# Block-product chunks: where the down slabs stand, where the raw blocks lie, and which sums a transfer makes

## The chip, the core and the metric

The kernel runs on one core of a Trainium2 chip. The core has a matrix engine (PE, with its weight loads shown apart as PEld), a vector engine (DVE), a scalar engine (ACT), a general engine (POOL) and a queue engine (SP) that here only issues transfers. Sixteen DMA engines move data between the chip's memory and the core's SBUF. The metric is the device time of one execution in microseconds. A program's instructions stand in one fixed order on each engine; engines wait for each other on semaphores.

## The reference

Two layers are computed on 256 tokens of width 1024, in float32. Each layer is a feed-forward part, a mixer (short convolution, recurrence, pooling), cross attention to 256 memory rows, and a second feed-forward part, each followed by a normalisation:

```
def swiglu(x, w_gate, w_up, w_down):
    return (jax.nn.silu(x @ w_gate) * (x @ w_up)) @ w_down
...
for l in range(DEPTH):
    h = layer_norm(ALPHA * h + 0.5 * swiglu(h, ffn1_gate[l], ffn1_up[l], ffn1_down[l]), ...)
    ... mixer, cross attention ...
    h = layer_norm(ALPHA * h + 0.5 * swiglu(h, ffn2_gate[l], ffn2_up[l], ffn2_down[l]), ...)
```

The gate and up weights are 1024 x 2816, the down weights 2816 x 1024. So there are four feed-forward parts, and they are what the change touches.

## The kernel before

**Products.** To keep float32 accuracy with the faster float32r matmul, each operand is split into a high part and a rest: `split` copies the value to float32r on ScalarE (L61) and subtracts it on VectorE (L62). A product is three matmuls, high by high, high by rest, rest by high (`mm_rows`, L112 by `product`). Weights come by transfers from SP into tiles of 128 x 1024 numbers with the tag `raw` (six of them) and are split into tiles `whi` and `wlo`, eight of each.

**A feed-forward part** (`ffn`) goes over the 2816 columns in five chunks of 512 and one of 256. For a chunk it computes gate and up, applies silu, multiplies, and turns the result (`turn`: four transfers named `dealt` that move it between partitions, two vector transposes at L458, one more split into `ah` and `al`). The chunk's result is then multiplied with rows of the down weights. Those come as two slabs of 256 rows for each chunk; `both(c, u)` makes the 24 matmuls of slab u of chunk c, into four PSUM banks that stay open for the whole part. The slabs lag behind: around chunk c stand `both(c - 2, 1)` and `both(c - 1, 0)`.

**Block products.** Chunks 2, 3 and 4 of a part (only 3 and 4 of the first part of layer 0, where other work is done at the start: `sevens`) are computed by `by_seven`. The chunk is seen as a 2 by 2 product: token halves by halves of the 1024 inner rows, times the gate block and the up block, each in two halves of rows: `w00` and `w10` are the gate's first and second half, `w01` and `w11` the up's. Seven products of blocks instead of eight give the result. Some of them take sums of blocks: the sums of x are made once a part (`blocks_of_x`, `bx`), the sums of weight blocks in each chunk, in place in the raw tiles, by `parts_of(r, plus)` at L606: two VectorE additions of 128 x 1024 for a block. Each product (`run`) has 12 matmuls. In this order the kernel before makes: x00 by w00; bx0 by w00+w01; bx1 by that plus w11; (x01) by w10; bx2 by w01+w11; then `between()`, which is `both(c - 2, 1)`; bx3 by w11; x11 by the sum of all four. Three sums are thus made: the first two add into w00 on VectorE, the third adds w11 into w01 on VectorE. The fourth block of the last sum, w10, is added into w00 by accumulating transfers from POOL's queue (L644): they read the gate's second half from memory again and add it to what lies in SBUF. After the seventh product stands `both(c - 1, 0)`, and then `left()`: silu of the second token half, the last subtraction, the gating product at L664, and `turn`.

Results of products are taken from PSUM by `taken` (a ScalarE copy, L635) and `put` (a VectorE operation, L625).

**Where raw blocks lie.** A block needs two raw tiles. Besides the six shared `raw` tiles there are `spare0`, `spare1` and `spare2` of the part's own pool, and `lng` and `lnb`, which hold normalisation parameters at the end of each part. Chunks alternate: w00 lies in the spares and w01 in lng/lnb, or the other way round; w11 takes two shared tiles, w10 `spare2` and one shared tile. A load into a tile is issued from SP when the last reader of the tile's old content is done, and SP's loads are issued in one order.

**What sets the order.** The code is recorded by a framework that keeps the order of dependent work and orders each engine's instructions by its own estimates of when they can start. So an engine's order is fixed in the built program, but isn't the code's line by line; the order of PE is nearly that of the code, while VectorE and ScalarE go ahead into the next products and into the next chunk as far as the eight tiles of split weights let them.

Of the kernel before, what the change touches and what calls it, by code (L numbers as in the profile page):

```python
# [12 lines left out]
ALU = mybir.AluOpType  # L13
# [4 lines left out]
P = 128  # L18
# [10 lines left out]
CHUNK = 512  # L29
# [17 lines left out]
def model(ctx: ExitStack, tc: tile.TileContext, t: dict, out: bass.AP):  # L47
    nc = tc.nc
# [5 lines left out]
    def acc(shape=(P, 2, SEQ), tag="acc"):  # L54
        return ps.tile(list(shape), F32, tag=tag, name=tag)
# [351 lines left out]
    def ffn(l, name, n, pend=None, last=False, early=None):  # L407
        gate, up, down = (t[f"{name}_{x}"][l] for x in ("gate", "up", "down"))
        with tc.tile_pool(name="ffn", bufs=2, reuse_waits="tile") as fp:
# [165 lines left out]
            def by_seven(c0, bx, between):  # L575
# [19 lines left out]
                homes = [("spare0", "spare1"), ("lng", "lnb")]  # L595
                turn_of = sevens.index(c0 // CHUNK) % 2
                w00 = block(gate, 0, pieces(*homes[turn_of]))
                w01 = block(up, 0, pieces(*homes[1 - turn_of]))
                w11 = block(up, 1, pieces("raw", "raw"))
                w10 = block(gate, 1, pieces("spare2", "raw"))  # L600

# [28 lines left out]
                s = activations()  # L630
# [6 lines left out]
                o = [acc((P, CHUNK)) for _ in range(2)]  # L637
                run(o[0], part_of_x(0, 0), parts_of(w00))
                taken(s[:, 0, :], o[0])
                run(o[1], bx[0], parts_of(w00, w01))  # L640
                run(o[0], bx[1], parts_of(w00, w11), True)
                for i in range(2):
                    k = 4 + 2 * i
                    nc.gpsimd.dma_start(  # L644
                        w00[i], gate[k * P : (k + 2) * P, c0 : c0 + CHUNK].rearrange("(k p) c -> p k c", p=P),
                        accum_op=ALU.add,
                    )
                taken(e, o[0])
                o.append(acc((P, CHUNK)))
                run(o[2], part_of_x(0, 1), parts_of(w10))  # L650
                run(o[0], bx[2], parts_of(w01, w11), True)
                put(s[:, 0, :], o[2], ALU.add, s[:, 0, :])
                nc.scalar.activation(s[:, 0, :], s[:, 0, :], AF.Silu)
                taken(f, o[0])
                between()
# [71 lines left out]
            for c, (c0, ncol) in enumerate(chunks):  # L727
# [3 lines left out]
                elif c in sevens:  # L731
                    left = by_seven(c0, bx, lambda: both(c - 2, 1))
# [16 lines left out]
                if c > 0:  # L749
                    if c > 1 and c not in sevens:  # L750
                        both(c - 2, 1)
                    if c < len(chunks) - 1:
                        both(c - 1, 0)
                    if c in sevens:
                        acts.append(left())
            end = [slab(4, 0), slab(4, 1), slab(5, 0)]
# [479 lines left out]
```

## Time and profile before

| | |
|---|---|
| Median of three runs | 1084.16 us (1083.94 to 1084.78) |
| The profiled execution | 1086.89 us |
| Its span, first to last instruction | 1085.2 us |
| Granted TensorE clock, mean | 0.997 |
| Busy: PE, DVE, ACT, POOL | 1059.0, 969.0, 669.1, 91.5 us |
| Read from memory | 227.69 MB |

The page gives for each group of instructions its line and engine, what it writes and reads, how often it stands, its busy time, the mean of one in ns, and the idle time before it with what ended it. The chain of waits follows the work that ended last back to the start. The windows give busy times inside stretches of the span. Matmuls are pipelined, so a matmul's own time overlaps the next one's; how far apart their starts are tells their price.

### The profile page before, as it was taken

What the parts mean: (1) busy time and instruction counts of PE and PEld (TensorE: products, weight loads), DVE (VectorE), ACT (ScalarE), POOL (GpSimd) and SP (SyncE); (2) the same over time, 40 slices, a digit from 0 to 9 for tenths busy, and PEclk for the clock granted to TensorE, in tenths of its full rate; (3) what the DMA queues carried; (4) which work ended last, traced back from release to release, by engine and by line L of the source; (5) the groups of instructions that cost most, each with busy time, mean ns of one, the idle gap of its engine ahead of it and who ended that gap; (6) DMA issues with size and microseconds to landing.
All of it is one profiled execution on the core that took longest, in us unless ns stands there. A gap on an engine that the chain in (4) does not pass through costs nothing.

```text
span 1085.2 us, 16259 instructions
## 1 busy us (share of the span) xinstructions
PE 1059.0 (98%) x5918; PEld 927.8 (85%) x5918; DVE 969.0 (89%) x1279; ACT 669.1 (62%) x920; POOL 91.5 (8%) x136
## 2 busy tenths in 40 slices
PE   9998999999999999999999999999999999999997
PEld 7887788989899888888888887888898998888786
DVE  6979987998998799999899999888989788999996
ACT  7547675767457566567575677666764655667661
POOL 9600001000000000000000000010000000000000
PEclk9999999999999999999999999999999999999999
DMA  9997595755575587679776787957536664786691
GB/s 361 266 290 209 160 322 181 254 195 166 165 271 176 177 278 201 209 259 268 237 276 191 270 271 190 300 181 241 182 131 210 240 238 166 252 271 192 196 291 40
DMA packets 136882, 243.45 MB, mean 224 GB/s; under 512 B 9761, under 2 KB 48961, under 8 KB 136801
## 3 DMA queue, kind: packets, MB, share of 16 engines
q1 hardware_dynamic: 129024, 228.49, 62.4%
q0 software_dynamic: 7200, 12.73, 7.0%
q10 hardware_dynamic: 576, 1.18, 0.3%
q8 instruction: 46, 0.75, 0.3%
q14 instruction: 36, 0.29, 0.1%
HBM read 227.69 MB, written 1.05 MB: 211 GB/s over the span
## 4 chain that ended last, share of the span: by engine, by line
PE 69%; DVE 15%; DMA 7%; issue 5%; ACT 3%; SPq 0%; DVEq 0%; ACTq 0%
PE acc L112 45%; PE dn L112 21%; DVE wlo L62 8%; DMA raw<-in_ffn_up_dram 3%; DMA raw<-in_ffn_gate_dram 3%; DVE raw L606 3%; ACT whi L61 2%; DMA dealt<-sg 1%; PE acc L179 1%; DVE square L458 1%; DVE sg L664 1%; PE dn L938 1%; DVE al L62 1%; DVE sg L445 0%; SPq L455 0%
## 5 line engine op out<-in xcount | busy, mean ns | idle before, releaser
L61 ACT CAST whi<-raw 128x1024 fp32r<-128x1024 f32 (+1 forms) x462 | 463.7, 1041 | 184.4 <-DVE raw L606 79.0
L62 DVE TENSOR_TENSOR wlo<-raw,whi 128x1024 fp32r<-128x1024 f32 (+1 forms) x462 | 542.5, 1207 | 27.2 <-ACT whi L61 24.4
L112 PE MATMUL acc<-whi,xT 128*128 128x512 f32 x872 | 268.5, 381 | 5.0 <-ACT whi L61 4.8
L112 PEld LDWEIGHTS acc<-whi,xT 128*128 128x128 f32 x872 | 164.9, 189 | 30.5 <-ACT whi L61 7.4
L112 PE MATMUL acc<-wlo,xT 128*128 128x512 f32 x436 | 165.8, 380 | 3.5 <-DVE wlo L62 3.5
L112 PE MATMUL acc<-xT,whi 128*128 128x512 f32 x576 | 142.2, 382 | 0.2
L112 PE MATMUL dn<-whi,ah 128*128 128x512 f32 x346 | 130.1, 381 | 1.4 <-ACT whi L61 1.4
L112 PE MATMUL dn<-wlo,ah 128*128 128x512 f32 x346 | 131.4, 380 | 0.0
L112 PE MATMUL dn<-whi,al 128*128 128x512 f32 x346 | 131.1, 379 | 0.0
L112 PEld LDWEIGHTS acc<-xT,whi 128*128 128x128 f32 x576 | 104.0, 190 | 12.5 <-ACT whi L61 0.7
L112 PEld LDWEIGHTS acc<-wlo,xT 128*128 128x128 f32 x436 | 82.4, 189 | 16.8 <-DVE wlo L62 5.4
L112 PE MATMUL dn<-whi,xT 128*128 128x512 f32 x288 | 87.8, 381 | 0.0
L606 DVE TENSOR_TENSOR raw<-raw 128x1024 f32<-128x1024 f32 x66 | 78.7, 1215 | 1.7 <-DMA raw<-in_ffn_up_dram 1.6
L112 PEld LDWEIGHTS acc<-xT,wlo 128*128 128x128 f32 x576 | 75.5, 191 | 3.9
L112 PE MATMUL acc<-xT,wlo 128*128 128x256 f32 x576 | 75.9, 275 | 0.0
L112 PEld LDWEIGHTS dn<-whi,ah 128*128 128x128 f32 x346 | 65.1, 189 | 12.0 <-ACT whi L61 3.0
L112 PE MATMUL acc<-whi,kTh 128*128 128x512 f32 x176 | 68.5, 389 | 5.8 <-ACT sg L635 3.8
L112 PEld LDWEIGHTS dn<-wlo,ah 128*128 128x128 f32 x346 | 65.4, 189 | 10.0 <-DVE wlo L62 0.9
L112 PEld LDWEIGHTS dn<-whi,al 128*128 128x128 f32 x346 | 65.4, 189 | 9.2
L112 PE MATMUL acc<-wlo,kTh 128*128 128x512 f32 x176 | 67.7, 385 | 0.8 <-DVE wlo L62 0.8
L112 PE MATMUL acc<-whi,kTl 128*128 128x512 f32 x176 | 67.5, 383 | 0.0
L112 PEld LDWEIGHTS dn<-whi,xT 128*128 128x128 f32 x288 | 54.4, 189 | 7.7 <-DVE xT L62 0.3
(235 smaller groups left out, 1297.0 us busy)
## 6 DMA issues: line engine op xcount, KB each, us to landing
raw<-in_ffn_up_dram SPq DMA_DIRECT2D x88, 512.0 KB, 5.8
raw<-in_ffn_down_dram SPq DMA_DIRECT2D x88, 512.0 KB, 5.7
raw<-in_ffn_gate_dram SPq DMA_DIRECT2D x84, 512.0 KB, 5.3
raw<-in_w_in_dram SPq DMA_DIRECT2D x48, 512.0 KB, 4.7
raw<-in_ffn_gate_dram POOLq DMA_DIRECT2D x22, 512.0 KB, 6.4
dealt<-sg SPq DMA_DIRECT2D x80, 128.0 KB, 3.2
raw<-in_ca_k_dram SPq DMA_DIRECT2D x16, 512.0 KB, 4.9
raw<-in_w_out_dram SPq DMA_DIRECT2D x16, 512.0 KB, 4.4
```

The lines of the kernel that those rows point to most:

```text
L61: nc.scalar.copy(hi, src)
L62: lows.append(nc.vector.tensor_tensor(lo, src, hi.bitcast(F32), op=ALU.subtract))
L112: nc.tensor.matmul(o, w, x, start=start, stop=stop, skip_group_check=more)
L179: nc.tensor.transpose(pt[:, k, :], src[:, (4 * j + k) * P : (4 * j + k + 1) * P], unit)
L458: nc.vector.transpose(d[:, i].rearrange("p k (b r) -> p b k r", b=4), x[:, :, i, :].rearrange("p b (k j) -> p b k j", k=4),)
L606: nc.vector.tensor_tensor(r[i], r[i], plus[i], op=ALU.add)
L664: nc.vector.tensor_tensor(s, s, ef, op=ALU.mult)
L938: nc.tensor.matmul(o[g, hh, :], kc[:, hh, g], x, start=True, stop=True)
```

## The change

Four things change inside `by_seven` and around it.

1. The third sum, w01 + w11, is no longer made on VectorE. A function `more` issues accumulating transfers; it is used for w00 as before, and now also for w01: after the sum w00 + w01 has read it, two transfers from POOL's queue add the up's second half into it.
2. The order of products. x01 by w10 now stands third, into its own bank that is there from the start, and bx1 by w00+w01+w11 fourth. The next slab product `both(c - 2, 1)` then stands between the fourth product and bx2 by w01+w11, which add to one bank; and `both(c - 1, 0)` stands between that one and bx3 by w11. `left()` follows the seventh product at once.
3. The raw blocks lie in three homes by turns, the spares, lng/lnb and two shared tiles, so that w00, w01 and w11 move on by one home from chunk to chunk.
4. The gate's second half (w10) is loaded ahead of the up's second half (w11).

The number of matmuls, of splits and of plain loads is the same.

```diff
-                homes = [("spare0", "spare1"), ("lng", "lnb")]
-                turn_of = sevens.index(c0 // CHUNK) % 2
-                w00 = block(gate, 0, pieces(*homes[turn_of]))
-                w01 = block(up, 0, pieces(*homes[1 - turn_of]))
-                w11 = block(up, 1, pieces("raw", "raw"))
+                homes = [("spare0", "spare1"), ("lng", "lnb"), ("raw", "raw")]
+                n = sevens.index(c0 // CHUNK)
+                w00 = block(gate, 0, pieces(*homes[n % 3]))
+                w01 = block(up, 0, pieces(*homes[(n + 1) % 3]))
                 w10 = block(gate, 1, pieces("spare2", "raw"))
+                w11 = block(up, 1, pieces(*homes[(n + 2) % 3]))
...
-                o = [acc((P, CHUNK)) for _ in range(2)]
+                o = [acc((P, CHUNK)) for _ in range(3)]
                 run(o[0], part_of_x(0, 0), parts_of(w00))
                 taken(s[:, 0, :], o[0])
+                def more(to, m, j):
+                    for i in range(2):
+                        k = 4 * j + 2 * i
+                        nc.gpsimd.dma_start(
+                            to[i], m[k * P : (k + 2) * P, c0 : c0 + CHUNK].rearrange("(k p) c -> p k c", p=P),
+                            accum_op=ALU.add,
+                        )
+
                 run(o[1], bx[0], parts_of(w00, w01))
+                more(w01, up, 1)
+                run(o[2], part_of_x(0, 1), parts_of(w10))
                 run(o[0], bx[1], parts_of(w00, w11), True)
-                for i in range(2):
-                    k = 4 + 2 * i
-                    nc.gpsimd.dma_start(
-                        w00[i], gate[k * P : (k + 2) * P, c0 : c0 + CHUNK].rearrange("(k p) c -> p k c", p=P),
-                        accum_op=ALU.add,
-                    )
+                more(w00, gate, 1)
+                put(s[:, 0, :], o[2], ALU.add, s[:, 0, :])
                 taken(e, o[0])
-                o.append(acc((P, CHUNK)))
-                run(o[2], part_of_x(0, 1), parts_of(w10))
-                run(o[0], bx[2], parts_of(w01, w11), True)
-                put(s[:, 0, :], o[2], ALU.add, s[:, 0, :])
+                between[0]()
                 nc.scalar.activation(s[:, 0, :], s[:, 0, :], AF.Silu)
+                run(o[0], bx[2], parts_of(w01), True)
                 taken(f, o[0])
-                between()
+                between[1]()
                 put(f, o[1], ALU.subtract, f)
                 run(o[1], bx[3], parts_of(w11), True)
                 run(o[0], part_of_x(1, 1), parts_of(w00), True)
...
-                    left = by_seven(c0, bx, lambda: both(c - 2, 1))
+                    left = by_seven(c0, bx, [lambda: both(c - 2, 1), lambda: both(c - 1, 0)])
...
-                    if c > 1 and c not in sevens:
-                        both(c - 2, 1)
-                    if c < len(chunks) - 1:
-                        both(c - 1, 0)
                     if c in sevens:
                         acts.append(left())
+                    else:
+                        if c > 1:
+                            both(c - 2, 1)
+                        if c < len(chunks) - 1:
+                            both(c - 1, 0)
```

## The prediction

> **What bounds the kernel now.** I read the page first, for the busiest engine and the chain of waits, then the windows of the stretches that the change touches, then the timeline inside them.
>
> ```profile
> span 1085.2 us, 16259 instructions
> PE 1059.0 (98%) x5918; PEld 927.8 (85%) x5918; DVE 969.0 (89%) x1279; ACT 669.1 (62%) x920; POOL 91.5 (8%) x136
> PE 69%; DVE 15%; DMA 7%; issue 5%; ACT 3%; SPq 0%; DVEq 0%; ACTq 0%
> ```
> ```profile
> 161.29 18.13 PE dn L112 x84
> ```
> TensorE is the bound, and no matmul is taken away or added. The chain's undisturbed run gives the price of a 128x512 matmul, 18.13 / 84 = 0.2158 us. What can be won is only what PE loses. A block-product chunk has seven products of 12 matmuls and two down slabs of 24, so 132 x 0.2158 = 28.5 us. These windows run from the first matmul of a feed-forward part's first such chunk to the last matmul of its last one (two chunks in the first part, three in the others):
>
> ```profile
> 85.79:150.65 64.86, 59.47 (x266) 50.83 (x264) 64.54 (x76) 46.73 (x53) 4.85 (x4) 0.97 0.74 223
> 421.25:512.60 91.35, 87.90 (x398) 74.11 (x397) 88.44 (x85) 64.10 (x73) 5.95 (x5) 1.00 0.82 248
> 592.17:684.25 92.08, 87.92 (x397) 74.11 (x396) 88.91 (x86) 63.96 (x73) 5.99 (x5) 1.00 0.82 245
> 954.85:1046.27 91.42, 87.93 (x397) 74.11 (x396) 89.52 (x86) 63.92 (x73) 5.96 (x5) 1.00 0.81 247
> ```
> Columns after the length: busy PE, PEld, DVE, ACT, POOL, then clock, share of the DMA engines, GB/s. Against 264 x 0.2158 = 57.0 and 396 x 0.2158 = 85.5 us, PE loses 7.9, 5.9, 6.6 and 6.0: 26.4 us together, the ceiling of any gain. Who takes them: the timeline of PE, and the chain between 440 and 492 us.
>
> ```profile
> 94.49 0.48 PE L112 MATMUL acc<-whi,kTh 128*128 128x512 f32 x1 [3.35 <-ACT sg L635]
> 96.27 0.63 PE L112 MATMUL acc<-whi,kTh 128*128 128x512 f32 x1
> 96.70 0.63 PE L112 MATMUL acc<-wlo,kTh 128*128 128x512 f32 x1
> 457.85 0.48 PE L112 MATMUL acc<-wlo,xT 128*128 128x512 f32 x1 [0.96 <-DVE wlo L62]
> 659.54 0.48 PE L112 MATMUL acc<-whi,xT 128*128 128x512 f32 x1 [2.01 <-ACT whi L61]
> ```
> ```profile
> by line: DVE wlo L62 38.8%; issue 19.8%; DMA raw<-in_ffn_up_dram 11.3%; DVE raw L606 10.1%; DMA raw<-in_ffn_gate_dram 8.6%; DVE square L458 4.8%; DVE sg L664 4.7%; PE acc L112 3.1%; DVE al L62 2.2%; ACT whi L61 2.0%; DVE halves L625 1.3%; D
> ```
> PE waits for the splits of weights into hi and lo, and their chain is VectorE's: splits (L62) and block sums (L606). After the longest wait ten matmuls came 0.43 us apart, so that one cost some 2 us more.
>
> **The change part by part.** First VectorE's price of a chunk.
>
> ```profile
> L606 DVE TENSOR_TENSOR raw<-raw 128x1024 f32<-128x1024 f32 x66 | 78.7, 1215 | 1.7 <-DMA raw<-in_ffn_up_dram 1.6
> ```
> ```profile
> 498.82 0.68 DVE L625 TENSOR_TENSOR halves<-acc,halves 128x512 f32<-128x512 f32 x1
> 499.42 6.89 DVE L62 TENSOR_TENSOR wlo<-raw,whi 128x1024 fp32r<-128x1024 f32 x6
> ```
> ```profile
> 457.72 1.30 DVE square L458 x2
> ```
> Large instructions follow each other at (6.89 - 1.22) / 5 = 1.135 us, those from PSUM at 0.60, the two transposes take 1.3. Now a chunk has 6 sums, 14 block splits, 4 slab splits, the gating product and one split of the activations: 26 x 1.135 + 3 x 0.60 + 1.3 = 32.6 us, 4.1 above PE. With the third sum made by transfers it is 24, or 30.3 us: 1.85 above PE. VectorE is still the slower one, but starts ahead. What it starts with is read from the loss: 3 x 4.1 - 5.9 = 6.4 us (5.7 and 6.3 in the later parts). Three chunks then use up 5.6 of it, and the loss is gone. In the first part 7.9 less 2 of slow clock is 5.9, so the start is 8.2 - 5.9 = 2.3; two chunks need 3.7, and 1.4 stays.
>
> The order. Until now five products come before the first slab, with 16 of the large instructions against 60 matmuls (18.2 against 12.9 us); then four products, 12 against 48 (13.6 against 10.4), and each slab (2.3 against 5.2) lets VectorE catch up sooner. In the built program the split of the earlier chunk's activations, which the second slab now needs before the sixth product, stands behind 21 large instructions, three small and the transposes, 27 us into VectorE's chunk, and PE is there after 5 x 2.59 + 5.18 = 18.1. So 8.8 us of lead are needed. Eight buffers of split weights let VectorE be up to the splits of the second sum ahead (13 large, two small, 16 us in the new order), so 7.2 are to spare against 5.6 used. I book no gain for the order, since the loss is used up already.
>
> ```profile
> q1 hardware_dynamic: 129024, 228.49, 62.4%
> q0 software_dynamic: 7200, 12.73, 7.0%
> raw<-in_ffn_up_dram SPq DMA_DIRECT2D x88, 512.0 KB, 5.8
> raw<-in_ffn_gate_dram POOLq DMA_DIRECT2D x22, 512.0 KB, 6.4
> ```
> ```profile
> L644 POOL DMA_DIRECT2D raw<-in_ffn_gate_dram x22 | 26.4, 1202 | 385.8 <-DVE wlo L62 385.8
> ```
> ```profile
> DMA to landing us min/median/max: 5.6/6.4/8.9
> ```
> ```profile
> DMA to landing us min/median/max: 3.6/5.8/8.3
> ```
> The last two are of the accumulating transfers (L644) and of the chunks' raw loads (L590).
> The transfers. 22 more accumulating ones. POOL's issue (1.2 us each) is free: it waits 385.8 us in that place. The gate block's transfers stand behind the up block's on that queue, whose last is released by a sum that VectorE does some seven instructions earlier. In the built order ten large instructions, two small and the transposes (13.8 us) lie between the sum that last reads the up block and its split, and ten, one and the transposes (13.2) between the second sum's split and the last product's; the slowest landing took 8.9, so both are hidden, with 4 us to spare. On the engines one costs at most 7.0% of 1085.2 us / 22 = 3.45 us of all sixteen (the queue carries other things too) and at least what a plain one costs, 62.4% x 1085.2 / 228.49 MB x 0.524 = 1.55. I take 3.1, near the upper row, since those are the same transfers.
>
> Homes. The up block of a next chunk no longer lies where the last product's weights were, but where the up block's second half was. Its buffer comes free one product earlier; in a third chunk five large VectorE instructions and a small one (6.3 us) lie between that and its sum, against a landing of 5.8. At 8.3 it would be 2 us late, at 3.6 not at all: I take 1 us in each part for this and for restarts, 4 in all. The gate's second half is loaded ahead of the up's, as it is now used first. The third bank is taken from the start: four exist, three were used, no cost. The gating starts right after the seventh product, with the next chunk's first product as cover (2.6 us against 0.6 of activation for the bank); behind the gating multiply queue the next chunk's later splits, which wait for buffers then anyway; without that cover 1 us a chunk.
>
> Sum: 26.4 - 1.4 - 4 = 21.0 us. The profiled execution took 1086.89 (1.7 around its span), the median of the runs is 1084.16, 2.7 less: 1065.9 profiled, 1063.2 for the median.
>
> **The rivals.**
>
> ```profile
> 430.00:442.00 12.00, 11.48 (x53) 9.75 (x52) 11.44 (x11) 9.27 (x11) 0.00 (x0) 1.00 1.05 407
> 445.00:454.00 9.00, 9.00 (x43) 7.87 (x43) 9.00 (x9) 2.69 (x3) 0.57 (x1) 1.00 0.25 61
> 490.00:496.00 6.00, 5.74 (x25) 4.48 (x25) 6.00 (x7) 6.00 (x8) 1.20 (x1) 1.00 1.03 173
> 492.00:524.00 32.00, 32.00 (x164) 27.90 (x163) 29.42 (x30) 22.12 (x28) 0.00 (x0) 1.00 0.99 308
> ```
> One: the DMA engines become the bound. The second part's 0.82 x 91.35 = 74.9 us get 6 x 3.1 more: 93.5. At the highest share seen, 1.05, that is 89.1 us, not 85.5; the three long parts win 2.3, 3.0 and 2.3, the first 7.4, and the time is 1069. At 0.99 it is 94.4 us, each long part loses 3 and the kernel ends near 1089. For it: accumulates alone fill the engines (1.03) at 173 GB/s. Against it: the engines stand at 0.25 where the new ones start, and at 0.99 for 32 us PE lost nothing.
> The Trainium skill ("DMA: Bandwidth & Descriptors", Issuing engines are not separate DMA queues) says that transfers from every queue run on the same 16 engines and interleave, which speaks for this rival; the trace agrees, 1.05 at most for both queues together. By the same page's fit (Anatomy of one DMA, 2.0 us and bytes at 436 GB/s) an accumulate would hold them 1.2 us as an estimate, and the second part would need 82.1 / 1.05 = 78.2, no bound; the trace's 173 GB/s for accumulates alone contradicts that.
>
> Two, slower: the second slab waits. It stands two products earlier and needs the earlier chunk's activations, whose way is:
>
> ```profile
> 418.43 2.62 SPq L455 DMA_DIRECT2D dealt<-sg  x4
> ```
> ```profile
> dealt<-sg SPq DMA_DIRECT2D x80, 128.0 KB, 3.2
> ```
> ```profile
> L61 ACT CAST ah<-square 128x1024 fp32r<-128x1024 f32 x20 | 20.9, 1046 | 14.1 <-DVE square L458 14.1
> L441 ACT ACTIVATE sg<-acc 128x512 f32<-128x512 f32 x27 | 15.9, 594 | 23.0 <-PE acc L112 22.0 <-DMA dealt<-sg 0.9
> ```
> Activation 0.6, multiply 1.2, issues 2.6, landing 3.2, transposes 1.3, cast 1.0, split 1.2: 11.1 us against PE's 18.1. It decides if the lead never reaches 8.8: from 26.4 / 11 = 2.4 us of wait a chunk on, the kernel is slower, and a wait as long as the 3.35 seen also slows the clock. At 3.5 a chunk: +38.5 - 26.4, or 1096.
> Three, nothing moves: PE's waits are for loads, so VectorE's sums don't matter. The chain's 20% of raw loads speak for it, L606 in the same chain against it: 1084.
>
> **How the numbers follow.** Forecast 0.60 (own range 1059 to 1068, from no slip to a slip of 2 us in each part more); DMA-bound and still faster 0.15 (1069 to 1081); no change, that is within 0.2% or 2.2 us, which is what a measurement of this kernel can tell, 0.05; DMA-bound at 0.99 0.07 (1089); waiting slab 0.13 (1096). Faster 0.75, same 0.05, slower 0.20. The range goes from 1058, all 26.4 us won, to 1087, short of the slower cases.
>
> **What would show it.** L606 x44, VectorE's busy time 27 us less, 44 accumulates, the software queue near 24.3 MB; the long parts' windows at 86 to 87.5 us and the first at 58 to 60, DMA share there 0.95 and above. Landings of raw loads over 7 us in the median, or new PE waits of dn matmuls for the activations' splits, would make it wrong.

## The result and the profile after

The changed kernel takes 1078.73 us (median, 1078.14 to 1081.95), the kernel before 1084.88 us (1083.94 to 1087.26) on the same chip: the ratio is 0.9946, with a 95% interval of 0.993 to 0.9962. It is faster by 4 to 8 us. The forecast was 1063.2 us, a gain of 21 us; the direction came, less than a third of the size did.

The page of the changed kernel: the span, the busy engines, the chain by engines, the software queue, the sums and the accumulating transfers.

```profile
span 1076.9 us, 16377 instructions
PE 1056.5 (98%) x5918; PEld 925.8 (86%) x5918; DVE 947.1 (88%) x1257; ACT 671.2 (62%) x920; POOL 119.0 (11%) x158
q0 software_dynamic: 13184, 24.27, 13.2%
PE 69%; DVE 14%; DMA 6%; issue 6%; ACT 5%; SPq 1%; DVEq 0%; ACTq 0%
L606 DVE TENSOR_TENSOR raw<-raw 128x1024 f32<-128x1024 f32 x44 | 53.0, 1218 | 0.4
raw<-in_ffn_up_dram POOLq DMA_DIRECT2D x22, 512.0 KB, 6.0
raw<-in_ffn_gate_dram POOLq DMA_DIRECT2D x22, 512.0 KB, 7.9
```

The profiled execution took 1078.62 us, within 0.1 us of the median of its kernel; that of before had been 2 us above its own. What was to be removed is removed: 22 additions fewer, 44 accumulating transfers, 24.27 MB in the software queue. VectorE is 22 us less busy, where 27 were forecast. TensorE's share did not move, as it was the bound already.

The windows of the same four stretches, from the first matmul of a part's first block-product chunk to the last of its last one (columns as in the prediction: length, PE, PEld, DVE, ACT, POOL, clock, DMA share, GB/s):

```profile
85.49:147.87 62.38, 58.48 (x265) 49.49 (x264) 60.47 (x72) 46.63 (x53) 7.15 (x6) 1.00 0.94 265
419.45:508.47 89.02, 86.92 (x398) 74.37 (x396) 84.26 (x81) 62.14 (x71) 11.95 (x10) 1.00 0.98 269
588.48:677.08 88.60, 86.92 (x397) 74.30 (x396) 83.88 (x80) 61.57 (x69) 11.91 (x10) 1.00 0.98 270
948.29:1036.90 88.61, 86.93 (x398) 74.30 (x397) 83.88 (x80) 61.34 (x70) 11.91 (x10) 1.00 0.98 268
```

Against the floors of 57.0 and 85.5 us TensorE (264 and 396 matmuls of 0.2158 us) now loses 5.4, 3.6, 3.1 and 3.1 us, 15.2 in all where it was 26.4: 11.2 us are won here. The span fell by 8.3 only, so some 3 us came back outside. The distances between the stretches show where: from the end of one to the start of the next it was 270.60, 79.57 and 270.60 us, and is 271.58, 80.01 and 271.21; from the end of the last one to the end of the span it was 38.9 us and is 40.0. Right behind each stretch stands a new wait: matmuls of a down slab need the activations (ah) of the 256-column chunk. In the kernel before, a slab still stood behind the seventh product, and these activations were ready in time. At the four places the matmuls' starts now lie 1.0, 0.4, 0.4 and 1.2 us further apart than the price of a matmul, 3.0 us together; before, no start there was late. The waits of TensorE, and its timeline at the first of these places:

```profile
PE dn L112 <- ACT whi L61: 3.3, 4, 0.9
PE dn L112 <- DVE wlo L62: 2.6, 7, 1.0
PE acc L112 <- ACT halves L635: 1.8, 2, 1.6
PE acc L112 <- ACT sg L635: 1.6, 4, 0.8
PE dn L112 <- ACT ah L61: 0.9, 2, 0.6
```
```profile
167.93 0.48 PE L112 MATMUL dn<-whi,ah 128*128 128x512 f32 x1 [0.36 <-ACT ah L61]
```

The rows of waits give the sum in us, the number and the longest. Those for the activations sum to 0.9 us, less than the 3.0 above, since a wait is counted here only from 0.1 us on and the matmul after it is late too. No wait is long, and four kinds remain: for the cast of slab weights, for their split, for the copies that ScalarE makes of the products' banks (L635, `taken`), and for the activations behind the stretch.

The first two are the largest, 5.9 us. In the third chunk of the second part:

```profile
486.94 1.13 PE L112 MATMUL dn<-whi,ah 128*128 128x512 f32 x4 [0.80 <-ACT whi L61]
484.90 4.84 ACT L61 CAST whi<-raw 128x1024 fp32r<-128x1024 f32 x5 [4.17 <-DVE raw L606]
```

The slab's cast stands on ScalarE behind the cast of a block sum, and ScalarE has stood idle for 4.17 us until VectorE had made that sum. VectorE in turn waits 1.17 us for the cast before it can split. All four of TensorE's waits for casts of slab weights stand right behind such an idle time of ScalarE, of 4.17 to 5.40 us. So VectorE sets the pace there without being busy throughout. No run takes this hand-over away by itself, so what it is worth is not shown.

One more thing is only in the trace. The written order puts the first slab between the fourth product and the fifth. In the built program, from the second block-product chunk of a part on, 13 to 16 of that slab's 24 matmuls stand ahead of the fourth product: the scheduler filled a gap with them. Which gap, the timeline of TensorE shows in the second such chunk of the second part, where 0.76 us of it are left:

```profile
459.43 0.38 PE L112 MATMUL dn<-whi,ah 128*128 128x512 f32 x1
460.56 0.48 PE L112 MATMUL acc<-whi,kTh 128*128 128x512 f32 x1 [0.76 <-ACT sg L635]
```

The fourth product adds to the bank of the first, so it waits until ScalarE has copied that bank into the tile `sg`. This became the centre of the study.

### The profile page after: what moved, and what is told of

The parts are those of the page before. It is cut to its first block, busy times and chain, and to the rows that moved or that the text cites. A ratio compares the mean times of both kernels' runs of the same rounds, so it can differ in the third digit from the quotient of the medians.

```text
span 1076.9 us, 16377 instructions
## 1 busy us (share of the span) xinstructions
PE 1056.5 (98%) x5918; PEld 925.8 (86%) x5918; DVE 947.1 (88%) x1257; ACT 671.2 (62%) x920; POOL 119.0 (11%) x158
## 3 DMA queue, kind: packets, MB, share of 16 engines
q0 software_dynamic: 13184, 24.27, 13.2%
## 4 chain that ended last, share of the span: by engine, by line
PE 69%; DVE 14%; DMA 6%; issue 6%; ACT 5%; SPq 1%; DVEq 0%; ACTq 0%
PE acc L112 47%; PE dn L112 20%; DVE wlo L62 6%; ACT whi L61 4%; DMA dealt<-sg 2%; DVE raw L606 2%; DMA raw<-in_ffn_gate_dram 1%; DMA raw<-in_ffn_up_dram 1%; PE acc L179 1%; SPq L455 1%; DVE square L458 1%; DMA raw<-in_ffn_down_dram 1%; DVE sg L668 1%; PE dn L943 1%; ACT ah L61 0%
## 5 line engine op out<-in xcount | busy, mean ns | idle before, releaser
L357 POOL TENSOR_TENSOR rs<-rs,nhalf 128x1 f32<-128x1 f32 x16 | 14.9, 933 | 434.0 <-DVE rs L353 307.1
```

The lines of the kernel that those rows point to most:

```text
L357: nc.gpsimd.tensor_tensor(rs, rs, nhalf[:, 0:1], op=ALU.pow)
```

## The experiments

All times are medians; ratios are to the kernel before on the same chip, with 95% intervals. The kernel before took 1084.9 to 1086.2 us beside the various runs, so differences between two changed kernels are taken from their ratios.

**First round: three suspicions.** Theory A was that the order built for TensorE, with slab matmuls ahead of the fourth product, costs what is missing; B that the DMA engines became full; C that the cover lost behind the stretches costs it. The first kernel holds TensorE to the written order:

```
+                    with tc.manual_schedule(engines={E.PE}):
-                    left = by_seven(c0, bx, [lambda: both(c - 2, 1), lambda: both(c - 1, 0)])
+                        left = by_seven(c0, bx, [lambda: both(c - 2, 1), lambda: both(c - 1, 0)])
```

> The changed kernel, with PE's instructions of each block-product chunk kept in the order in which they are written: in the changed kernel the built order puts 13 to 16 of the first slab's matmuls ahead of the fourth product in second and third chunks. Theory A (PE's built order asks for the slab's splits and for the fourth product's bank sooner than VectorE and ScalarE deliver them): the long parts' stretches fall from 89.0, 88.6 and 88.6 us to 87 or less and the first from 62.4 to 60 or less, the time by 4 to 8 us against the changed kernel, to 1071 to 1075. Theory B (the DMA engines, 0.98 busy there, set the pace): the stretches keep within 0.7 us of these lengths, PE's waits only stand in other places, the time stays 1077 to 1080.

It took 1114.33 us, 1.0258 (1.0244 to 1.0271): 34 us slower than the changed kernel, the opposite of A. TensorE's waits, and its timeline at one of them:

```profile
PE acc L112 <- ACT sg L635: 33.2, 7, 6.1
```
```profile
466.15 0.48 PE L112 MATMUL acc<-whi,kTh 128*128 128x512 f32 x1 [4.20 <-ACT sg L635]
467.33 0.61 PE L112 MATMUL acc<-whi,kTl 128*128 128x512 f32 x1
467.73 0.63 PE L112 MATMUL acc<-whi,kTh 128*128 128x512 f32 x1
```

Seven fourth products wait 33.2 us for the copy of the first product's bank, up to 6.1 each, and behind such a wait matmuls come 0.40 us and more apart instead of 0.216 for a while. The slab matmuls ahead of the fourth product had not cost this time but covered it.

The second kernel puts the last block-product chunk's second slab back behind its seventh product:

```
-                    left = by_seven(c0, bx, [lambda: both(c - 2, 1), lambda: both(c - 1, 0)])
+                    second = (lambda: None) if c == max(sevens) else (lambda: both(c - 1, 0))
+                    left = by_seven(c0, bx, [lambda: both(c - 2, 1), second])
...
                     if c in sevens:
+                        if c == max(sevens):
+                            both(c - 1, 0)
                         acts.append(left())
```

> The changed kernel, with the second slab of a part's last block-product chunk put back behind that chunk's seventh product; the other chunks as changed. Theory C (without that slab the 256-column chunk's activations must wait for the buffer that the gating result still leaves, and its end comes late): the waits of 0.5 to 1.2 us behind the stretches at 168, 528, 697 and 1056 us, 3 us in all, go, and the time falls by 1.5 to 3 us against the changed kernel. Theory B (late slab loads of full DMA engines make these waits): they stay, and the time is within 1 us of the changed kernel's.

1086.42 us, 0.9994 (0.9979 to 1.001): all the gain is gone. The waits for ah behind the stretches are gone too, as C has it, but larger ones stand ahead of the fifth product, which adds to the bank of the fourth and waits for its copy:

```profile
PE acc L112 <- ACT halves L635: 9.2, 5, 3.2
```

In the two longest of these, 2.8 and 3.2 us, the copy stands on ScalarE behind a cast that had waited 2.2 and 2.7 us for a raw block of the gate; why that block comes later here is not shown. So C names a real cost, 3 us, and its remedy costs 5 more than it wins. The third kernel is the kernel before with one part of the change alone, the third sum by adding transfers:

```
                 run(o[1], bx[0], parts_of(w00, w01))
+                for i in range(2):
+                    k = 4 + 2 * i
+                    nc.gpsimd.dma_start(
+                        w01[i], up[k * P : (k + 2) * P, c0 : c0 + CHUNK].rearrange("(k p) c -> p k c", p=P),
+                        accum_op=ALU.add,
+                    )
...
-                run(o[0], bx[2], parts_of(w01, w11), True)
+                run(o[0], bx[2], parts_of(w01), True)
```

> The kernel before, with only the third sum made by accumulating transfers; order of products and homes as before. By the lead account of the prediction (VectorE's 2.27 us a chunk pay for the whole loss): about 1064. If it is the order that brought the measured gain: within 2 us of the kernel before, 1083 to 1086. If both share it: 1077 to 1081, like the changed kernel.

1082.59 us, 0.9975 (0.9965 to 0.9985). This is the run that breaks the forecast's account. VectorE sheds all 22 additions, in the order in which the account was drawn up, and only some 3 us come. The windows of its long stretches, and TensorE's waits:

```profile
419.22:510.80 91.58, 87.21 (x398) 74.36 (x397) 86.78 (x83) 63.97 (x73) 10.83 (x9) 1.00 0.97 278
590.29:681.30 91.01, 87.43 (x398) 74.37 (x397) 87.09 (x84) 64.31 (x73) 10.80 (x9) 1.00 0.98 279
951.79:1041.20 89.41, 86.96 (x398) 74.57 (x397) 87.24 (x84) 64.24 (x73) 10.80 (x9) 1.00 0.98 283
```
```profile
PE acc L112 <- ACT sg L635: 12.9, 9, 2.0
PE acc L112 <- DVE wlo L62: 1.0, 3, 0.3
```

VectorE now stands idle for 2.2 to 4.8 us of each stretch (1.9 to 3.2 in the kernel before), and TensorE still loses 6.1, 5.5 and 3.9, where it had lost 5.9, 6.6 and 6.0. The waits for VectorE's splits are nearly gone (1.0 us), and the wait for the copy of the first product's bank has taken their place (12.9 us). What that copy waits for, ScalarE's timeline shows:

```profile
425.08 0.58 ACT L635 COPY sg<-acc 128x512 f32<-128x512 f32 x1 [1.96 <-DMA dealt<-sg]
```

The copy writes the tile `sg`, from which the transfers `dealt` still read the earlier chunk's activations. In eight of the eleven chunks it starts 0.1 us after the last of these transfers has landed (in three in the kernel before). In five of the eight ScalarE stood idle for it, in the other three its casts ended at the same moment. Of the 12.9 us the eight account for 8.6, the five alone for 4.6. The fourth kernel is the changed one without the new transfers; it leaves the up block's second half out of the third sum, so that its time shows what the transfers cost and nothing else:

```
-                more(w01, up, 1)
```

> The changed kernel without the new transfers: the up block's second half isn't added into the third sum, so that sum lacks it and the result is another. VectorE, PE and ScalarE do the same as in the changed kernel. Theory B (DMA engines full): the share in the stretches falls from 0.98 to about 0.80 and the time by 4 us or more, to 1074.5 or less. Theory A (PE's order): the same waits of PE stay and the time is within 1.5 us of the changed kernel's 1078.7.

1079.10 us, 0.9941 (0.9929 to 0.9953): within 0.6 us of the changed kernel, although the share of the DMA engines in the long stretches falls from 0.98 to between 0.82 and 0.84. The transfers are hidden, and B falls.

**Second round: the parts, and the copy.** Two theories were set against each other: F, the products wait for ScalarE's copies of banks; G, VectorE's amount of work sets the pace. First the change without its transfers (sum on VectorE again) and the change with two homes:

```
-                more(w01, up, 1)
-                run(o[0], bx[2], parts_of(w01), True)
+                run(o[0], bx[2], parts_of(w01, w11), True)
```

> The changed kernel with the third sum made by VectorE again (w01 + w11 before the fifth product) and without the transfers that add the second half of the up block; order and homes stay the changed ones. Theory F (bank copies: what is lost in a stage is the wait of a product for ScalarE's copy of the bank it adds to, and the slab in the gap covers it, whoever makes the sum): the order brings its part alone, what the transfers alone did not bring: 1085.8 - (1085.8 - 1078.9) + 3.2 = about 1082, 1080.5 to 1083.5. Theory G (VectorE's amount of work sets the pace of the long stretches: it is busy 83.9 of 88.6 us there): with two sums more in each chunk, 2.4 us, a long stretch takes 88.6 + 3 x 2.4 = 95.8 less the idle time of 4.7, about 91, as before: 1085 to 1088.

```
-                homes = [("spare0", "spare1"), ("lng", "lnb"), ("raw", "raw")]
-                n = sevens.index(c0 // CHUNK)
+                homes = [("spare0", "spare1"), ("lng", "lnb")]
+                n = sevens.index(c0 // CHUNK) % 2
...
-                w11 = block(up, 1, pieces(*homes[(n + 2) % 3]))
+                w11 = block(up, 1, pieces("raw", "raw"))
```

> The changed kernel with the raw blocks on two homes in turn, the fourth block always in the two shared buffers, as before; order and transfers stay. Theories F and G both: the homes move transfers only, and no product waits for a raw block in the long stretches: 1077.5 to 1080. Rival (the third home lets a block start earlier and this carries part of the gain): 1081 to 1084, with TensorE or VectorE waiting for a raw block of the up matrix.

The first took 1102.69 us, 1.016 (1.0145 to 1.0175), beyond both ranges; the second 1092.07 us, 1.0064 (1.0051 to 1.0077), the rival's mechanism at some three times its size. VectorE's waits with two homes:

```profile
DVE raw L606 <- DMA raw<-in_ffn_up_dram: 12.1, 8, 3.1
```

All eight waits are of a chunk's first sum, w00 + w01. With two homes w01 is loaded to where the chunk before had its w00, which the seventh product uses last, and it lands up to 3.1 us too late. That the new order makes this worse than the old one, as no slab stands between the seventh product and the next chunk any more, is read from the code and not shown by itself. In the first run TensorE's largest wait is for casts of slab weights (13.7 us), and VectorE's waits for blocks of the up matrix sum to 6.5. The third home, booked in the prediction as a cost within 1 us a part, is worth 13 us there.

Next came the copy of the first product's bank. In the kernel with the written order it stood behind seven casts on ScalarE; so the casts for the fourth product were issued behind it:

```
-                taken(s[:, 0, :], o[0])
+                first = taken(s[:, 0, :], o[0])
...
-                run(o[0], bx[1], parts_of(w00, w11), True)
+                with tc.issue_after(first.ins):
+                    w = parts_of(w00, w11)
+                run(o[0], bx[1], w, True)
```

> The kernel with TensorE in the written order (1114.3 us), with one thing more: ScalarE's casts for the fourth product are issued behind its copy of the first product's bank, so that the copy no longer stands behind them. Theory F: the seven waits of the fourth products for that copy (33.2 us together, about 4.4 to 6.2 each) go to under 4 us together, and the time falls by 28 to 36 us to 1078 to 1086. Theory G: TensorE then waits for the weights of the fourth product's sum instead, 3 us or more at each, and the time stays over 1095.

1132.46 us, 1.0441 (1.0428 to 1.0454): G's range by the number, since TensorE waits for the high parts of weights. But these are late because ScalarE's casts stand behind the copy now, and the copy waits. ScalarE's waits:

```profile
ACT sg L635 <- DMA dealt<-sg: 84.0, 9, 11.9
```

The copy couldn't go earlier there, as its target wasn't free. There is one tile `sg`. It holds the earlier chunk's activations times up, from where four transfers (L455) deal them out, and until the last has landed the next first product can't be copied into it. The changed kernel shows it in the chunk above, once one knows where to look. Its tile `dealt` between 449 and 463 us, and ScalarE's timeline there:

```profile
L455 SPq DMA_DIRECT2D dealt<-sg x4: 615/634/666, 450.5 to 452.5; - x4
DMA to landing us min/median/max: 4.8/5.3/7.3
```
```profile
452.81 6.73 ACT L61 CAST whi<-raw 128x1024 fp32r<-128x1024 f32 x7 [4.08 <-DVE raw L606]
459.92 0.59 ACT L635 COPY sg<-acc 128x512 f32<-128x512 f32 x1 [0.38 <-ACT whi L61]
```

The last transfer is issued at 452.5 and lands 7.3 us later, at 459.8; the copy starts at 459.92, the fourth product at 460.56. The seven casts end at 459.54, so the last 0.4 us of the wait that the profile puts down to ScalarE are one for a transfer that sets a buffer free. In the other three such waits of this kernel (0.27 us each) the transfer had landed 0.2 us or more before the copy, which came straight behind the casts.

The last kernel of the round moves the two remaining sums to GpSimd:

```
-                            nc.vector.tensor_tensor(r[i], r[i], plus[i], op=ALU.add)
+                            nc.gpsimd.tensor_tensor(r[i], r[i], plus[i], op=ALU.add)
```

> The changed kernel with both remaining sums of each block-product chunk (44 additions of two 512 KB pieces) on GpSimd in place of VectorE. Theory G: VectorE sheds 4 x 1.13 = 4.5 us a chunk, 13.6 us of a long stretch, and is idle a fifth of it; the losses of the long stretches fall from 3.1 - 3.6 us to under 1.5, and the time to 1069 - 1074. Theory F: ScalarE's idle time of 4.1 us ahead of a sum's cast goes as well, the copy of the bank comes earlier, the same range. Rival (GpSimd is slow at it or slows VectorE at the same memory: an addition takes over 3.5 us, or VectorE's splits grow over 1.3 us): 1078 to 1095, with new waits of ScalarE's casts for GpSimd.

1156.81 us, 1.0657 (1.0642 to 1.0672): the rival, and worse than its range. Groups by form:

```profile
L62 DVE TENSOR_TENSOR wlo<-raw,whi 128x1024 fp32r<-128x1024 f32 x454 | 603.7, 1363 | 87.4 <-ACT whi L61 77.0 <-PE acc L112 8.9
L606 POOL TENSOR_TENSOR raw<-raw 128x1024 f32<-128x1024 f32 x44 | 129.4, 2944 | 231.7 <-DVE wlo L62 181.8 <-DMA raw<-in_ffn_gate_dram 25.9 <-DMA raw<-in_ffn_down_dram 24.0
```

An addition takes 2.94 us instead of 1.22, and VectorE's splits grow from 1.217 (its mean in the changed kernel) to 1.363 us each, 66 us over 454 of them, more than the 54 us that it sheds (44 x 1.22). G stays untested by this. The Trainium skill ("GPSIMD Engine Reference", 3.1 Elementwise — side-by-side cycle accounting) gives about twice VectorE's time for such an addition; here it is 2.4 times, with VectorE at work beside it.

**Third round: the remaining parts, and the tile set free.** Two runs complete the table of parts. The old order with transfers and three homes is the third kernel above and this edit:

```
-                homes = [("spare0", "spare1"), ("lng", "lnb")]
-                turn_of = sevens.index(c0 // CHUNK) % 2
-                w00 = block(gate, 0, pieces(*homes[turn_of]))
-                w01 = block(up, 0, pieces(*homes[1 - turn_of]))
-                w11 = block(up, 1, pieces("raw", "raw"))
-                w10 = block(gate, 1, pieces("spare2", "raw"))
+                homes = [("spare0", "spare1"), ("lng", "lnb"), ("raw", "raw")]
+                n = sevens.index(c0 // CHUNK)
+                w00 = block(gate, 0, pieces(*homes[n % 3]))
+                w01 = block(up, 0, pieces(*homes[(n + 1) % 3]))
+                w10 = block(gate, 1, pieces("spare2", "raw"))
+                w11 = block(up, 1, pieces(*homes[(n + 2) % 3]))
```

> The kernel before with the third sum by adding transfers and with the blocks over three homes, in the old order: the change without its order. Theory I (the parts need each other: two homes cost 13.4 us beside order and transfers, the sum on VectorE 24 us beside order and homes, while the transfers alone bring 3.2): the order is what the other two are there for, and without it they bring what the transfers bring alone, 1081 to 1084. Rival K (the order is worth nothing or costs, and the other two alone would be better): 1074 to 1078.

1080.49 us, 0.9961 (0.9949 to 0.9973): half a us under the range of Theory I, far from that of K. The order alone is the changed kernel with this edit turned round and with the third sum on VectorE as in the second round:

> The changed kernel with two homes and with the third sum on VectorE: the order alone. Theory I: both costs of the incomplete change come together, 24 us and 13 us, partly the same wait (a sum that comes late): 1100 to 1118. Rival K: about 1090 to 1100, since two homes would cost nothing more where VectorE is late anyhow.

1113.74 us, 1.0266 (1.0252 to 1.0279), as I has it. Then the edit that the misplaced copy suggested: the product of gate and up goes over the halves, and `sg` is free when the multiplication ends.

```
-                    nc.vector.tensor_tensor(s, s, ef, op=ALU.mult)
-                    return turn(s)
+                    nc.vector.tensor_tensor(ef, s, ef, op=ALU.mult)
+                    return turn(ef)
```

> The changed kernel with one edit: the product of gate and up is written over the halves instead of over the activations, so that the transfers that deal it out read the halves' tile, and the activations' tile is free for the copy of the next first product at the end of the multiplication, 9.3 us earlier in the chunk at 450 us (450.45 in place of the landing at 459.78). Theory J (the fourth product waits for the copy, the copy for these transfers): the fourth product comes ahead of the slab again, its wait for that copy goes, and the losses of the three long stretches fall from 3.1 - 3.6 to 1.5 - 2.5 us each: 1072 to 1077. Theory G (VectorE's amount of work sets the pace): nothing to win, 1077.5 to 1080. Rival: the scheduler's other order brings waits of its own, over 1081.

> As the one before, with TensorE held to the written order besides, as in the run that took 1114.3 us. Theory J: of the 33.2 us that the fourth products waited there for the copy less than 8 are left, and the time is 1074 to 1086. Theory G: the waits go to the sums' weights instead, and the time stays over 1095.

With TensorE in the written order this takes the 1114.33 us of the first round to 1079.85, 0.995 (0.9938 to 0.9962): the edit to one buffer wins 33 us, and the waits for the copy into `sg` are off the list. So the held tile causes these waits. By which path, ScalarE's timeline in the kernel of the first round shows:

```profile
458.88 6.73 ACT L61 CAST whi<-raw 128x1024 fp32r<-128x1024 f32 x7 [4.08 <-DVE raw L606]
465.52 0.58 ACT L635 COPY sg<-acc 128x512 f32<-128x512 f32 x1
```

The last transfer that reads `sg` had landed 3.6 us before this copy. The copy is late because it stands behind seven casts in ScalarE's built order, the first of which waits 4.08 us for a block sum. So it is in five of the seven waits (landed 3.5 to 3.9 us before); in the other two the copy follows the landing by 0.1 us. With the tile free the built order has the copy ahead of these casts. The held tile thus acts mostly through the order that the scheduler builds for it. VectorE has a part in these waits too: in all seven ScalarE is idle for 4.07 to 5.40 us ahead of the casts, until a block sum is made.

But the halves' tile is now the one that is held, until the dealt activations are turned in it and split:

```profile
PE acc L112 <- ACT halves L635: 12.5, 8, 3.7
```

With the built order the edit alone takes 1085.22 us (1.0006, 0.9991 to 1.0021): against Theory J (the fourth product waits for the copy, the copy for the transfers, and freeing the tile wins this back) and as the rival has it. The scheduler now builds the fourth product ahead of the slab, and TensorE waits 6.6 us for the halves' copies and 7.0 for the activations' low parts instead.

**Fourth round: both tiles free.** The turned product gets a tile of its own, so that no copy waits for any transfer. Its 4 KB a partition are taken from the eight buffers of high weight parts:

```
-                d = fp.tile([P, NT, 4, P], F32, tag="up", name="square", bufs=1)
+                d = fp.tile([P, NT, 4, P], F32, tag="sq", name="square", bufs=1)
...
-                        h = wp.tile([P, 1024], F32R, tag="whi", name="whi", bufs=8)
+                        h = wp.tile([P, 1024], F32R, tag="whi", name="whi", bufs=7)
```

> The changed kernel with the product of gate and up written over the halves (as in the run with the activations' tile free early), and the turned product in a tile of its own, so that neither the first product's copy nor the fourth's waits for the dealing transfers and the split; its 4 KB a partition come from the high parts of the weights, seven buffers in place of eight. Theory J: the waits for sg and halves (ScalarE L635) of the long stretches go below 1 us each, these take 86.5 to 88 us, and the time is 1066 to 1074. Theory G: VectorE's 84 us of work and its waits keep the stretches at 88.5 to 90 us: 1076 to 1082. Rival: seven buffers cost more than the tile brings, over 1082, with ScalarE's casts waiting for TensorE.

> As e13, with TensorE held to the written order. Theory J: of the 12.5 us that the products waited for the copies of the halves in the run with one tile free (1079.9 us) less than 4 are left: 1067 to 1074. Theory G: as that run, 1077 to 1083.

> Transfers and three homes in the old order (1080.5 us), with both tiles free and seven high buffers. Theory J: of the 10.0 us of waits for the first product's copy there most go: 1071 to 1076, and the order's own worth is the difference to e13. Theory G: 1079 to 1083.

The three took 1081.05 us (0.9948, 0.9936 to 0.996), 1082.16 us (0.9957, 0.9946 to 0.9969) and 1086.18 us (1.0002, 0.9993 to 1.0012). The copies' waits are gone from the first two, and yet no time is won: both lie in the ranges of Theory G, and the third beyond both ranges, without a cause shown. Two more runs ask whether the buffer that paid for the tile took it back. One takes that buffer from the changed kernel and does nothing else; the other frees both tiles and pays with a low buffer (wlo 7, whi 8).

> The changed kernel with seven buffers in place of eight for the high parts of the weights, nothing else. Theory L (the buffer cost what the free tiles won): 1082 to 1087, 3 to 8 us slower than the changed kernel, with more of ScalarE's casts waiting for TensorE. Theory G: the buffer costs nothing that can be measured, 1078 to 1081.

> Both tiles free as in e13, with eight high and seven low buffers. Theory L: the long stretches fall under 88 us, the time is 1069 to 1076. Theory G: they stay at 89 to 90 us, and the time at 1078 to 1083, since VectorE has as much to do as before and ends last in each of them.

The buffer alone costs 16 us, more than either theory had: 1096.23 us, 1.0092 (1.0077 to 1.0108). So the free tiles had won some 15 us beside it. But paid with a low buffer they bring 1079.78 us, 0.9941 (0.9929 to 0.9954), no better than the changed kernel and in the range of G. What the low buffer costs by itself was not measured. That kernel's windows and waits:

```profile
86.35:143.50 57.15, 57.15 (x266) 50.06 (x265) 55.59 (x68) 43.90 (x50) 7.16 (x6) 1.00 0.95 275
417.15:506.44 89.29, 86.97 (x398) 74.69 (x397) 83.96 (x80) 61.42 (x70) 11.96 (x10) 1.00 0.96 266
587.05:675.63 88.58, 86.70 (x398) 74.76 (x397) 83.95 (x80) 61.08 (x70) 11.93 (x10) 1.00 0.98 268
949.17:1038.18 89.01, 86.96 (x398) 74.68 (x397) 83.86 (x80) 60.52 (x69) 11.92 (x10) 1.00 0.96 263
```
```profile
PE acc L112 <- DVE wlo L62: 6.8, 12, 0.8
PE acc L112 <- ACT whi L61: 2.1, 3, 0.7
```
```profile
587.00:611.00 24.00, 24.00 (x112) 21.01 (x112) 22.10 (x22) 17.34 (x20) 3.57 (x3) 1.00 1.01 303
611.00:635.00 24.00, 24.00 (x113) 21.01 (x112) 23.95 (x24) 19.57 (x23) 3.60 (x3) 1.00 0.99 241
635.00:659.00 24.00, 22.12 (x99) 18.20 (x98) 21.30 (x21) 12.05 (x15) 4.77 (x4) 1.00 0.92 232
```

The first stretch, of two chunks, runs at its floor of 57.1 us: its loss of 5.4 us went with the single tiles. The stretches of three chunks still lose 3.1 to 3.8 us, and the last three rows, of one of them in pieces, show where. TensorE is full for 48 us; VectorE, idle 1.9 us in the first piece, is full in the second, and in the third, where the third chunk begins, TensorE waits for casts and splits. So VectorE's lead seems to last two chunks and to give out in the third, as G says, with a part from the loads: in that piece VectorE also waits 1.5 us for a raw block of the up matrix, and 1.1 for a cast. What a lighter VectorE would win there is not shown, since the attempt to make it lighter made it slower.

The last part by itself, three homes in the kernel before:

> The kernel before with the blocks over three homes, nothing else. Theory I (the homes only serve the new order, where the fourth block's sum would wait for its transfer): within 0.3% of before, 1083 to 1088. Rival: the third home alone wins the 2 us that it won beside the transfers: 1082 to 1084.

1083.23 us, 0.9967 (0.9954 to 0.998): homes alone win something, but both ranges hold this time, and the 0.3% of Theory I lie inside the interval, so the run does not decide between them. The parts together, as ratios to the kernel before:

| | old order | new order |
|---|---|---|
| neither | 1 | 1.0266 |
| transfers | 0.9975 | 1.0064 |
| three homes | 0.9967 | 1.016 |
| both | 0.9961 | 0.9946 |

Transfers and homes win 4 us in the old order. The new order costs 29 us by itself, and with both beside it is worth 1.6 us, which the intervals (0.9949 to 0.9973 and 0.993 to 0.9962) don't separate from nothing.

## Why the prediction was right and wrong

The direction was right, and so were the bound, the ceiling of 26.4 us as the only thing to win, the work that goes (44 sums, 44 transfers, 24.27 MB), and the transfers' cover: landings of 6.0 and 7.9 us under the 13 worked out, and nothing won by leaving the new ones out. The price of an accumulate, taken as 3.1 us of all sixteen engines, was right: by the software queue's shares on the two pages it is (13.2% x 1076.9 - 7.0% x 1085.2) / 22 = 3.0. Rival One (the DMA engines) fell by the run without the new transfers, which gave up a share of 0.14 to 0.16 and won nothing. Rival Two (the second slab waits) did not take place: the waits for the activations, 0.9 us, stand behind the stretches and not before the sixth product. Such waits were named as a sign of being wrong, and so were windows beyond 87.5 us: they are 88.6 to 89.0, and the first is 62.4 where 58 to 60 was forecast. Rival Three fell with the gain.

The size was wrong by 15.5 us, 1078.7 against 1063.2. The stretches were to lose 5.4 us (1.4 and 4 for homes and restarts) and lost 15.2, which is 9.8. Some 3 us came back behind them, which the sum did not have. And the profiled execution was taken to be 2.7 us above the median, while that of the changed kernel was at it.

- The step that failed is "What it starts with is read from the loss", with "Three chunks then use up 5.6 of it, and the loss is gone." It took the whole loss for VectorE's surplus of work, as if VectorE were never idle, and fitted a lead to it. But the long windows have VectorE idle for 1.9 to 3.2 us before and for 4.7 to 4.8 after the change. The transfers alone, in the order of before, took the work away, and the loss of the long stretches went from 18.5 to 15.5 us in all: the next wait, for the copy into `sg`, stood right behind. In the changed kernel 3.1 to 3.6 us are lost in each long stretch, at casts and splits of slab weights behind a late block sum, and at that copy. The row of 3.35 us (ACT sg L635), which the prediction quoted and booked under VectorE's chain, was another case: there the transfers had landed 7.8 us before the copy.
- "The gating starts right after the seventh product, with the next chunk's first product as cover": the cover was worked out for the bank, not for the tile that the gating writes. The dealing transfers hold `sg` for 9.3 us in the chunk shown (450.5 to 459.8), and the next fourth product waits for it. The landing was taken as 3.2 us; in the changed kernel it is 4.3 in the median and 7.3 for the last one of that chunk. What is late next was asked of engines and banks, and not of this buffer.
- "I book no gain for the order": right in size (1.6 us, not separable from nothing), for a wrong reason. The loss is not used up; the order costs 29 us by itself, and only the transfers and the homes beside it win that back.
- Homes and restarts, "1 us in each part", 4 in all: for the homes the sign was wrong. They win some 3 us alone in the old order, and in the new one the change would have been slower than before without them, 1092 us.
- VectorE did start ahead, and by more than was fitted. The long windows hold only 12 of a part's 18 block sums before the change and 8 of 12 after it; the others are done before the stretch begins. By the count of 32.6 us a chunk, less the time busy in the window, the head start that was used up is an estimate of 97.8 - 88.4 = 9.4 us in the second part (6.4 were fitted); the difference is VectorE's idle time. After the change it is 90.9 - 84.3 = 6.6, more than the 5.4 needed to keep up with TensorE: the work would have fitted, the waits between the engines did not.

## What to carry to other kernels

When one engine seems to set the pace, list for each wait of the bound engine what stands right behind it, buffers as well as engines: a copy that "waits for ScalarE" may wait for a transfer that still reads its target. A lead fitted to a loss proves nothing about the loss; the trace must show the engine full all through. Before taking a buffer or a home away or adding one, look who prefetches through it: one of eight buffers cost 16 us here. And a part of a change that costs 29 us alone may be harmless beside two others.

## What was not expected of the hardware and the program

- An order built by the scheduler, which looked like a fault, covered 33 us of waits.
- Waits of 4 us cost more than themselves: behind the 4.20 us wait above matmuls came 0.40 us and more apart, and the granted clock was 0.54 from 467.3 to 471 us. The Trainium skill ("TensorE: Matmul & The Clock Gate", Part 1: The HAM clock gate) has the clock fall after about 3.4 us without work. The traces agree only roughly: behind the 0.76 us wait at 460.56 matmuls kept to 0.216, but in the kernel with seven high buffers a wait of 2.86 us, at 491.03, was enough, and the granted clock was 0.56 in the 3 us from 491 us on.
- Small edits move the whole. A tile freed earlier made the fourth product's place change and the time rise by 6.5 us, while the same edit under a fixed TensorE order won 33.
